# Odd layer of a two-layer backbone: three projection blocks take the scaled input before its norm, and the norm factor and shift are applied to their products

## Chip, core and metric

The kernel runs on one core of one Trainium2 chip. The core has five engines that each work through a queue of their own in a fixed order: PE (TensorE, matrix products), DVE (VectorE), ACT (ScalarE), POOL (GpSimd) and SP (SyncE, which here issues the DMAs). The metric is the time of one execution on the device in microseconds (us). Before the change the median of three runs is 2517.13 us; the runs lie between 2510.89 and 2518.06 us.

## What is computed

The model has two layers over 512 latent tokens and 256 context tokens with 2048 features. Only the odd layer's entry is touched. There the reference normalises every token, scales and shifts it with vectors that come from a conditioning input, and projects it:

```python
def rmsnorm(x, g):
    xf = x.astype(jnp.float32)
    y = xf * lax.rsqrt(jnp.mean(xf * xf, axis=-1, keepdims=True) + EPS)
    return (y * g.astype(jnp.float32)).astype(x.dtype)
...
h = rmsnorm(x, norm_g[l]) * (1.0 + scale) + shift
hc = rmsnorm(cx, norm_g[l]) * (1.0 + cscale) + cshift
...
u = h @ o_w_in[i]
uc = hc @ o_w_in[i]
```

The projections feed attention (mixer C: q and k with a norm per head and rotary angles; mixer D: low-rank attention), a SiLU gate, an output projection and a gated residual add. A final RMSNorm ends the model.

Since the norm factor is one number for each token, and the shift one vector for each of the two token groups, a projection can also be written as: norm factor times (scaled input times weight), plus (shift times weight).

## The kernel before

Features lie on the 128 partitions, tokens along the free axis (768 columns: 512 latent, 256 context). The 2048 features make 16 chunks `k`. Each float32 operand of a product is split into a high part, rounded to the type float32r, and the low rest; a product is three matmuls: high by high (L275), low input by high weight (L276), high input by low weight (L278). A weight block of 128 columns arrives as `wraw`; ACT casts it to `wh` (L256), and DVE subtracts to get `wl` (L215).

**End of the even layer.** `out_chunk` (L652 on) takes each finished block of the output projection, adds the residual on DVE (L656, L657, tile `nx`), squares it on ACT (L664), sums the squares on POOL (L669, `acc1`), multiplies it with the odd layer's scale on DVE (L666), and stores it to memory as `xad[k]` (L667). So `xad` holds the scaled input of the odd layer, not yet normalised.

**Norm factor.** `rstd_cols` (L240 products with ones on PE, L244 square root on ACT, L245 reciprocal on DVE) and `spread` (L220 on PE, L227 copies on DVE) turn the sums of squares into `rs1`, the factor of each token, on all partitions.

**First three blocks.** The loop over `k` at L700 loads `xad[k]` back as `xk` (L702) and calls `make_h` (L343): `xn = xk * rs1` (L345; on DVE for every third chunk, else on POOL), `h`, the rounded `xn + shift` (L350 on ACT, one instruction for latent and one for context), and `l`, the rest (L356 on DVE, again two). The pairs `h`, `l` of all chunks stay in `hT`, from which all later projections of the layer read. Within the same loop PE forms three blocks from each chunk as it comes: head group 0's key (K0) and value (V0), each with 512 latent and 256 context columns, and query head 0 (Q0), latent only. Their products stand in three J banks and in the S banks.

**Behind them.** K0's products are squared (ACT, L770 and L771), a norm factor of their own is formed (L240, L244, L245, L220) and applied (L782), then come rotary angles (L398, L399 on DVE, L400, L401 on POOL) and a split into `kh`, `kl`. V0 is transposed on PE (L450). Q0 goes the way of K0. Attention begins with the score products (L470, L474). PE fills gaps there with the next projections (a SiLU gate), which read `hT`.

Beside this, `mod_later` forms modulation vectors for the end of the layer: it loads `mraw`, and DVE adds up `macc` (L170, 15 instructions in this part of the program).

**What sets the order.** A scheduler lays out the program by a timeline that it simulates itself when the kernel is built. What it decides is one fixed order for each engine; on the chip an engine takes its instructions in that order and waits where an operand is missing. Tiles come from pools: `s3` has 11 buffers (`xk`, `xh`, `xl`, `nx`, `res` and others share them), `tm` has 3 (`xn`), J has 3 banks, T has 2.

Of the kernel before, what the change touches and what calls it, by code (L numbers as in the profile page):

```python
# [9 lines left out]
F32 = mybir.dt.float32  # L10
F32R = mybir.dt.float32r
AF = mybir.ActivationFunctionType
ALU = mybir.AluOpType
# [4 lines left out]
P = 128  # L18
D_MODEL = 2048
NCH = D_MODEL // P  # L20
SEQ = 512
CTX = 256
TOK = SEQ + CTX
# [18 lines left out]
def trunk_kernel(ctx: ExitStack, tc: tile.TileContext, T):  # L42
    nc = tc.nc
# [5 lines left out]
    sm = ctx.enter_context(tc.tile_pool(name="sm", bufs=6))  # L49
    dr = ctx.enter_context(tc.tile_pool(name="dr", bufs=1, space=DRAM))  # L50
    psj = ctx.enter_context(tc.tile_pool(name="psj", bufs=3, space=PSUM))
# [5 lines left out]
    sp = {}  # L57
# [5 lines left out]
        return pss.tile([P, 1024], F32, tag="S", name="S")  # L63

    def slot(name):
        return sp["s3"].tile([P, TOK], F32, tag="s3", name=name)

    def slotr(name):
        return sp["s3"].tile([P, TOK], F32R, tag="s3", name=name)

    def oslot(name):
        return sp["s3"].tile([P, TOK], F32, tag="o", name=name, bufs=2)
# [11 lines left out]
    xad = [dr.tile([P, TOK], F32, name=f"xad{j}") for j in range(NCH)]  # L84
# [15 lines left out]
    tp = pst.tile([P, 512], F32, name="T")  # L100
    nc.tensor.transpose(out=tp[:, :NV1], in_=vrow[:NV1, 0:P], identity=ident[:NV1, :NV1])
    nc.vector.tensor_copy(vcol, tp[:, :NV1])
    tp = pst.tile([P, 512], F32, name="T")
# [16 lines left out]
    modc = [const.tile([P, 3 * NCH, 2], F32, name=f"modc{l}") for l in range(2)]  # L120
# [71 lines left out]
    hT = []  # L192

    last_x = None
# [19 lines left out]
    def sub(o, a, h):  # L214
        nc.vector.tensor_tensor(o, a, h.bitcast(F32), op=ALU.subtract)  # L215
# [4 lines left out]
            nc.tensor.matmul(dst[:, P * i:P * i + P], lhsT=cols[:, 2 * t:2 * t + 1].broadcast_to([P, P]), rhs=ident,  # L220
                             start=True, stop=True)

    def spread(cols, dst):
        for ts in ((0, 1, 2, 3), (4, 5)):
            tp = psj.tile([P, 512], F32, name="J")
            spread_to(tp, cols, ts)
            nc.vector.tensor_copy(dst[:, P * ts[0]:P * ts[-1] + P], tp[:, :P * len(ts)])  # L227

    def jbank():
        return psj.tile([P, 512], F32, name="J")  # L230

    def tbank():
        return pst.tile([P, 512], F32, name="T")

    def rstd_cols(accs, ts, dim, name, bank=jbank):

        mp = bank()
        steps = [(a, t) for a in accs for t in ts]
        for i, (a, t) in enumerate(steps):
            nc.tensor.matmul(mp[:, 2 * t:2 * t + 2], lhsT=a[:, P * t:P * t + P], rhs=ones[:, 0:2],  # L240
                             start=(i == 0), stop=(i == len(steps) - 1))
        rs = sm.tile([P, 12], F32, name=name, bufs=2)
        n = 2 * len(ts)
        nc.scalar.activation(rs[:, :n], mp[:, :n], AF.Sqrt, bias=epsc, scale=1.0 / dim)  # L244
        nc.vector.reciprocal(rs[:, :n], rs[:, :n])  # L245
        return rs


    def wsplit(rv, nk):

        res = []
        for k0 in range(0, nk, 4):
            n = min(4, nk - k0)
            wh = wp.tile([P, 4, P], F32R, name="wh", bufs=4)
            wl = wp.tile([P, 4, P], F32R, name="wl", bufs=4)
            nc.scalar.copy(wh[:, :n, :], rv[:, k0:k0 + n, :])  # L256
            sub(wl[:, :n, :], rv[:, k0:k0 + n, :], wh[:, :n, :])
            res += [(wh[:, i, :], wl[:, i, :]) for i in range(n)]
        return res

    def wraw(w, col, k0, nk, raw=None):

        if raw is None:
            raw = wp.tile([P, 1024], F32, name="wraw", bufs=3)
        nc.sync.dma_start(raw[:, :nk * P], w[col // P][:, k0 * P:(k0 + nk) * P])
        return raw[:, :nk * P].rearrange("p (k c) -> p k c", k=nk)

    def mm_step(lat, cx, wk, xk, first, last, opens=True, closes=True, at=(0, 512)):


        wh, wl = wk
        xh, xl = xk
        regs = [(lat, *at)] + ([(cx, 512, 768)] if cx is not None else [])
        for o, c0, c1 in regs:
            nc.tensor.matmul(o, lhsT=wh, rhs=xh[:, c0:c1], start=first and (opens or o is lat), stop=False)  # L275
            nc.tensor.matmul(o, lhsT=wh, rhs=xl[:, c0:c1], start=False, stop=False)  # L276
        for o, c0, c1 in regs:
            nc.tensor.matmul(o, lhsT=wl, rhs=xh[:, c0:c1], start=False, stop=last and (closes or o is lat))  # L278
# [16 lines left out]
    for k in range(NCH):  # L295
# [3 lines left out]
        sq = ss if k == 0 else sp["ep"].tile([P, TOK], F32, name="e")  # L299
# [63 lines left out]
    w = T["ew"]  # L363
    s_start = sbanks()
# [38 lines left out]
    def etile(name):  # L403
        return sp["ep"].tile([P, TOK], F32, tag="e", name=name)
# [281 lines left out]
    for j in range(NCH):  # L686
# [4 lines left out]


    w = T["ow"]
    rs1 = etile("rs1")
    spread(rstd_cols((acc1, sq), range(6), D_MODEL, "rsx"), rs1)
    s_start = sbanks()
    odd_cols = (C_K0, C_V0, C_Q0)
    odd_ps = [(psj.tile([P, 512], F32, name="J"), s_start[:, 256 * i:256 * i + 256] if i < 2 else None)
              for i in range(3)]
    for k in range(NCH):  # L700
        xk = slot("xk")
        last_x = nc.sync.dma_start(xk, xad[k])  # L702
        hT[k] = make_h(1, k, xk, rs1, tmp("xn"), "mod")
        for i, (lat, cx) in enumerate(odd_ps):
            if k % 4 == 0:
                ws4[i] = wsplit(wraw(w, odd_cols[i], k, 4), 4)
            mm_step(lat, cx, ws4[i][k % 4], hT[k], k == 0, k == NCH - 1, opens=(i % 2 == 0), closes=(i % 2 == 1))

    def scaled(cols, f):
        nc.vector.tensor_scalar(cols[:, :8], cols[:, :8], f, None, op0=ALU.mult)  # L710
# [329 lines left out]
```

## Time and profile before

| what | value |
|---|---|
| median of the runs shown | 2517.13 us (2510.89 to 2518.06) |
| profiled execution, its own time | 2510.88 us |
| its span, first to last instruction | 2508.9 us |
| DVE, ACT, POOL busy | 1574.6, 1011.5, 248.9 us |
| DMA | 297.47 MB, mean 119 GB/s |

The span is the time from the profile's first instruction to its last; 2.0 us of the execution's own time lie around it. The clock that the throttle granted to PE is 0.985 on average. A row of the timeline has the start in us from the span's start, the length in us, engine, line, operation, what it writes and reads, how many instructions were merged, and in brackets how long the engine sat idle before it and what released it. A row of the groups has the shapes, the count, the summed busy time in us and the mean in ns, and behind the bar the idle time before them. A row by windows has a stretch, its length, and for each engine the busy time and the number of instructions; at the end stand the granted PE clock as a share of full speed, the busy share of the DMA engines and GB/s.

### The profile page before, as it was taken

Reading aid. Unit: us, or ns where it says so; the run is one execution under the profiler, and the core shown is the slowest. Engines: PE = TensorE matmul, PEld = TensorE weight load, DVE = VectorE, ACT = ScalarE, POOL = GpSimd, SP = SyncE. Lnnn points to the kernel's source line nnn. Section 1 sums busy time; section 2 is a strip of 40 time slices with the busy share of each in tenths; the row PEclk is TensorE's granted clock in tenths of the full one; section 3 lists DMA queues with packets and bytes.
Section 4 is the critical chain, followed back from the end, with each engine's and each line's share of the span. In section 5 each row is a group of like instructions: output and inputs, shape, how many; then the busy total and the mean of one; then the engine's idle time right before and its main releaser. Section 6 shows DMA issues by size and latency. Waiting matters only on the chain.

```text
span 2508.9 us, 36275 instructions
## 1 busy us (share of the span) xinstructions
PE 2408.6 (96%) x14214; PEld 2077.9 (83%) x14214; DVE 1574.6 (63%) x2795; ACT 1011.5 (40%) x1963; POOL 248.9 (10%) x160
## 2 busy tenths in 40 slices
PE   4899999999999999999989999899999999999998
PEld 2667888888888899989878888788888888888787
DVE  5377667656955787887466664757545335776534
ACT  3234454544444334324342222344434334554434
POOL 1111001001000101010001012300001011000010
PEclk9899999999999999999999999899999999999999
DMA  8762111111311343453425555425422221122234
GB/s 325 259 229 76 43 56 57 49 57 57 118 58 66 102 148 108 143 165 112 133 96 202 183 171 191 138 93 196 145 72 85 70 94 64 55 93 69 96 118 151
DMA packets 99082, 297.47 MB, mean 119 GB/s; under 512 B 11616, under 2 KB 12640, under 8 KB 98912
## 3 DMA queue, kind: packets, MB, share of 16 engines
q1 hardware_dynamic: 98912, 295.16, 34.7%
q8 instruction: 112, 1.84, 0.3%
q14 instruction: 58, 0.48, 0.1%
HBM read 269.16 MB, written 25.95 MB: 118 GB/s over the span
## 4 chain that ended last, share of the span: by engine, by line
PE 88%; DVE 5%; DMA 3%; issue 2%; ACT 1%; SPq 0%; ACTq 0%; DVEq 0%
PE J L275 22%; PE J L276 22%; PE J L278 22%; PE O L532 6%; PE S L474 4%; PE T L517 3%; PE S L470 3%; DMA mraw<-in_wm_dram 2%; DVE macc L170 1%; PE T L144 1%; PE J L178 1%; DVE l L356 1%; DVE wl L215 1%; PE T L240 1%; PE T L220 1%
## 5 line engine op out<-in xcount | busy, mean ns | idle before, releaser
L275 PE MATMUL J<-h,wh 128*128 128x512 f32 (+1 forms) x2224 | 786.0, 357 | 18.7 <-ACT h L350 11.8
L276 PE MATMUL J<-l,wh 128*128 128x512 f32 (+1 forms) x2224 | 766.8, 355 | 2.9 <-DVE l L356 1.8
L278 PE MATMUL J<-h,wl 128*128 128x512 f32 (+1 forms) x2224 | 706.6, 355 | 6.2 <-DVE wl L215 6.2
L256 ACT CAST wh<-wraw 128x512 fp32r<-128x512 f32 x492 | 303.9, 620 | 693.9 <-PE J L276 589.2
L215 DVE TENSOR_TENSOR wl<-wraw,wh 128x512 fp32r<-128x512 f32 x500 | 362.6, 729 | 338.7 <-ACT wh L256 325.2
L275 PEld LDWEIGHTS J<-h,wh 128*128 128x128 f32 x2224 | 421.2, 190 | 98.4 <-ACT h L350 12.9
L276 PEld LDWEIGHTS J<-l,wh 128*128 128x128 f32 x2224 | 423.5, 190 | 61.5 <-DVE l L356 3.5
L278 PEld LDWEIGHTS J<-h,wl 128*128 128x128 f32 x2224 | 388.3, 191 | 41.3 <-DVE wl L215 7.7
L170 DVE SCALAR_TENSOR_TENSOR macc<-mraw,silc,macc 128x512 f32<-128x512 f32 x420 | 319.7, 792 | 28.6 <-DMA mraw<-in_wm_dram 26.2
L275 PE MATMUL J<-yh,wh 128*128 128x512 f32 (+1 forms) x800 | 276.1, 351 | 5.1 <-ACT yh L438 5.1
L276 PE MATMUL J<-yl,wh 128*128 128x512 f32 (+1 forms) x800 | 272.2, 350 | 1.1 <-DVE yl L215 0.9
L486 DVE TENSOR_REDUCE nb<-S 128x1 f32<-128x768 f32 (+3 forms) x208 | 166.2, 799 | 146.8 <-PE S L474 79.2
L278 PE MATMUL J<-yh,wl 128*128 128x512 f32 (+1 forms) x800 | 254.1, 349 | 0.0
L521 ACT CAST pth<-T 128x256 fp32r<-128x256 f32 (+2 forms) x288 | 125.3, 451 | 188.2 <-PE T L517 185.1
L275 PEld LDWEIGHTS J<-yh,wh 128*128 128x128 f32 x800 | 150.1, 189 | 32.1 <-ACT yh L438 5.9
L215 DVE TENSOR_TENSOR ptl<-T,pth 128x256 fp32r<-128x256 f32 (+2 forms) x288 | 144.2, 514 | 51.6 <-ACT pth L521 49.9
L276 PEld LDWEIGHTS J<-yl,wh 128*128 128x128 f32 x800 | 150.7, 189 | 22.5 <-DVE yl L215 3.3
L493 ACT ACTIVATE e<-S,nb 128x256 f32<-128x256 f32 (+3 forms) x144 | 104.4, 725 | 154.2 <-DVE nb L486 88.0
L278 PEld LDWEIGHTS J<-yh,wl 128*128 128x128 f32 x800 | 140.6, 189 | 12.6
L400 POOL TENSOR_TENSOR r<-r,cos 128x512 f32<-128x512 f32 x31 | 44.4, 1431 | 792.4 <-DVE t L399 737.7
L517 PE MATMUL T<-identr,e 128*128 128x128 f32 x784 | 115.5, 274 | 2.9 <-DVE e L503 2.6
L517 PEld LDWEIGHTS T<-identr,e 128*128 128x128 f32 x784 | 94.6, 141 | 16.6 <-issue 2.6
(283 smaller groups left out, 3137.5 us busy)
## 6 DMA issues: line engine op xcount, KB each, us to landing
mraw<-in_wm_dram SPq DMA_DIRECT2D x128, 512.0 KB, 3.6
wraw<-in_ew_dram SPq DMA_DIRECT2D x96, 512.0 KB, 3.5
wraw<-in_ow_dram SPq DMA_DIRECT2D x64, 512.0 KB, 3.6
wraw<-in_wo_dram SPq DMA_DIRECT2D x62, 512.0 KB, 3.8
mraw<-in_wm_dram SPq DMA_DIRECT2D x80, 384.0 KB, 7.4
xT<-in_xT_dram SPq DMA_DIRECT2D x16, 384.0 KB, 7.3
res<-in_xT_dram SPq DMA_DIRECT2D x16, 384.0 KB, 4.5
xad<-nx SPq DMA_DIRECT2D x16, 384.0 KB, 2.5
```

What stands on the lines that cost most here:

```text
L170: nc.vector.scalar_tensor_tensor(macc[:, v, :], rv[:, i, :], sc, macc[:, v, :], op0=ALU.mult, op1=ALU.add)
L215: nc.vector.tensor_tensor(o, a, h.bitcast(F32), op=ALU.subtract)
L256: nc.scalar.copy(wh[:, :n, :], rv[:, k0:k0 + n, :])
L275: nc.tensor.matmul(o, lhsT=wh, rhs=xh[:, c0:c1], start=first and (opens or o is lat), stop=False)
L276: nc.tensor.matmul(o, lhsT=wh, rhs=xl[:, c0:c1], start=False, stop=False)
L278: nc.tensor.matmul(o, lhsT=wl, rhs=xh[:, c0:c1], start=False, stop=last and (closes or o is lat))
L474: nc.tensor.matmul(S[:, 512:end], lhsT=q, rhs=k[:, 128 * lo:128 * hi], start=(i == 0), stop=(i == n - 1 and not masks))
L486: nc.vector.tensor_reduce(nb, S, axis=AX.X, op=ALU.max, negate=True)
L493: nc.scalar.activation(e, S, AF.Exp, bias=nb, scale=1.0 if scale is None else scale, accum_out=den)
L517: nc.tensor.transpose(out=tp[:, 128 * (b - b0):128 * (b - b0) + 128], in_=e[:, 128 * b:128 * b + 128], identity=ident)
L521: nc.scalar.copy(ph, tv)
L532: nc.tensor.matmul(o, lhsT=v[:, cols[i]], rhs=pt[part][:, i, :], start=(n == 0), stop=(n == len(steps) - 1))
```

## The change

The loop over `k` is split in two. The first loop reads `xad[k]` into a tile of 770 columns: 512 latent ones, then two columns that take the chunk's shift for latent and context from `modc`, then 256 context ones. The tile is split into `xh` and `xl` without norm and shift, and the three blocks are formed from these. The two extra columns of the product are shift times weight. Q0 gets the two columns in a T bank and is therefore formed as 256 and 258 columns. Behind the loop `rs1` is formed with T banks, and a new function `late_norm` multiplies each block by `rs1` on DVE out of the bank into an SBUF tile `first` and adds the shift's product on ACT. The second loop loads every `xad[k]` again and calls `make_h`, since all later projections still read `hT`; it forms no products.

```diff
+    def slot2(name, dt=F32):
+        return sp["s3"].tile([P, TOK + 2], dt, tag="s3", name=name)
...
-    spread(rstd_cols((acc1, sq), range(6), D_MODEL, "rsx"), rs1)
     s_start = sbanks()
     odd_cols = (C_K0, C_V0, C_Q0)
-    odd_ps = [(psj.tile([P, 512], F32, name="J"), s_start[:, 256 * i:256 * i + 256] if i < 2 else None)
-              for i in range(3)]
+    first_ps = [jbank() for _ in range(3)]
+    q_bank = tbank()
+    for k in range(NCH):
+        xk = slot2("xk")
+        last_x = nc.sync.dma_start(xk[:, 0:512], xad[k][:, 0:512])
+        nc.sync.dma_start(xk[:, 514:770], xad[k][:, 512:768])
+        nc.vector.tensor_copy(xk[:, 512:514], modc[1][:, k, :])
+        xh, xl = slot2("xh", F32R), slot2("xl", F32R)
+        nc.scalar.copy(xh, xk)
+        sub(xl, xk, xh)
+        for i in range(3):
+            if k % 4 == 0:
+                ws4[i] = wsplit(wraw(w, odd_cols[i], k, 4), 4)
+            wh, wl = ws4[i][k % 4]
+            if i < 2:
+                regs = ((first_ps[i], 0, 512), (s_start[:, 512 * i:512 * i + 258], 512, 770))
+            else:
+                regs = ((first_ps[i][:, 0:256], 0, 256), (q_bank[:, 0:258], 256, 514))
+            for n, (wk, xx) in enumerate(((wh, xh), (wh, xl), (wl, xh))):
+                for o, c0, c1 in regs:
+                    nc.tensor.matmul(o, lhsT=wk, rhs=xx[:, c0:c1], start=(k == 0 and n == 0),
+                                     stop=(k == NCH - 1 and n == 2))
+    spread(rstd_cols((acc1, sq), range(6), D_MODEL, "rsx", tbank), rs1, tbank)
+
+    def late_norm(name, parts, bias):
+        t = slot(name)
+        bc = sm.tile([P, 2], F32, name="bc", bufs=3)
+        nc.vector.tensor_copy(bc, bias)
+        for ps, c0, c1, v in parts:
+            nc.vector.tensor_tensor(t[:, c0:c1], ps, rs1[:, c0:c1], op=ALU.mult)
+            nc.scalar.activation(t[:, c0:c1], t[:, c0:c1], AF.Identity, bias=bc[:, v:v + 1])
+        return t
...
     for k in range(NCH):
         xk = slot("xk")
-        last_x = nc.sync.dma_start(xk, xad[k])
+        nc.sync.dma_start(xk, xad[k])
         hT[k] = make_h(1, k, xk, rs1, tmp("xn"), "mod")
-        for i, (lat, cx) in enumerate(odd_ps):
-            if k % 4 == 0:
-                ws4[i] = wsplit(wraw(w, odd_cols[i], k, 4), 4)
-            mm_step(lat, cx, ws4[i][k % 4], hT[k], k == 0, k == NCH - 1, opens=(i % 2 == 0), closes=(i % 2 == 1))
```

All tiles of `s3` grow by two columns. Up to the last chunk of the even layer the order of every engine is what it was. In the changed file the lines of functions ahead of this place stand three further down (L356 is now L359), those behind it 40 further down (L770 is now L810).

On DVE before, this is what stands between the last piece `l` of the sixteen chunks and the reciprocal (L245) for K0's own norm:

```order
L356 SCALAR_TENSOR_TENSOR l_15_15283<-xn,modc_194,h_15_15282 128x512
L356 SCALAR_TENSOR_TENSOR l_15_15283<-xn,modc_194,h_15_15282 128x256
L170 SCALAR_TENSOR_TENSOR macc<-mraw,silc,macc 128x512 x3
L215 TENSOR_TENSOR wl<-wraw,wh 128x512
L170 SCALAR_TENSOR_TENSOR macc<-mraw,silc,macc 128x512
L215 TENSOR_TENSOR wl<-wraw,wh 128x512 x2
L170 SCALAR_TENSOR_TENSOR macc<-mraw,silc,macc 128x512 x6
L215 TENSOR_TENSOR wl<-wraw,wh 128x512 x3
L245 RECIPROCAL rsx<-rsx 128x12
L782 TENSOR_TENSOR ev<-ev,T 128x512
```

On DVE after the change, the same reciprocal (now L248) stands behind the new multiplications (L732) and behind all sixteen `l`; the first gap leaves out the other multiplications and small rows, the second the `l` of the chunks between, five more `xn` and seven `macc`:

```order
L218 TENSOR_TENSOR xl<-xk,xh 128x770
...
L732 TENSOR_TENSOR first<-T,rs_14800 128x256
L173 SCALAR_TENSOR_TENSOR macc<-mraw,silc,macc 128x512
L218 TENSOR_TENSOR wl<-wraw,wh 128x512
L348 TENSOR_TENSOR xn<-xk,rs_14800 128x768
L173 SCALAR_TENSOR_TENSOR macc<-mraw,silc,macc 128x512 x2
L359 SCALAR_TENSOR_TENSOR l_0_15346<-xn,modc_194,h_0_15345 128x512
...
L359 SCALAR_TENSOR_TENSOR l_15_15496<-xn,modc_194,h_15_15495 128x256
L173 SCALAR_TENSOR_TENSOR macc<-mraw,silc,macc 128x512 x2
L248 RECIPROCAL rsx<-rsx 128x12
```

The sixteen pieces have moved from among the three blocks' products to behind them, and stay ahead of K0's norm.

On ACT after the change, the squares of K0 (L810, L811) stand behind all of `h`, and these behind the added shift (L733); the left-out rows are the `h` between:

```order
L733 ACTIVATE first<-first,bc 128x512
L733 ACTIVATE first<-first,bc 128x256 x3
L353 ACTIVATE h_0_15345<-xn,modc_194 128x512
...
L353 ACTIVATE h_15_15495<-xn,modc_194 128x256
L810 ACTIVATE sq<-first 128x512
L811 ACTIVATE sq<-first 128x256
L814 ACTIVATE ev<-first,vcol 128x512
```

Before, the squares stood behind all of `h` as well, but with no `L733`, and the products ran between.

On PE after the change, this is the end of the first loop's products (L722) and what follows:

```order
L722 MATMUL J<-xh,wl 128x256
L722 MATMUL T<-xh,wl 128x258
L243 MATMUL T<-ones,sq 128x2 x6
L223 MATMUL T<-identr,rsx 128x128 x6
L453 MATMUL J<-identr,ev 128x128 x6
L278 MATMUL J<-h_0_15345,wh 128x512
L279 MATMUL J<-l_0_15346,wh 128x512
```

Between the last product and K0's norm (L243, L223) nothing else stands on PE. Before, these rows followed the last of the blocks' products (L278) in the same way.

More of the change, by code (lines that the diff above doesn't have):

```diff
@@ L65, in slot @@
     def slot(name):
-        return sp["s3"].tile([P, TOK], F32, tag="s3", name=name)
+        return sp["s3"].tile([P, TOK + 2], F32, tag="s3", name=name)[:, :TOK]
+    def slot2(name, dt=F32):
+        return sp["s3"].tile([P, TOK + 2], dt, tag="s3", name=name)
     def slotr(name):
-        return sp["s3"].tile([P, TOK], F32R, tag="s3", name=name)
+        return sp["s3"].tile([P, TOK + 2], F32R, tag="s3", name=name)[:, :TOK]
     def oslot(name):
@@ L221, in spread_to, with spread @@
                              start=True, stop=True)
-    def spread(cols, dst):
+    def spread(cols, dst, bank=None):
         for ts in ((0, 1, 2, 3), (4, 5)):
-            tp = psj.tile([P, 512], F32, name="J")
+            tp = (bank or jbank)()
             spread_to(tp, cols, ts)
@@ new lines, in trunk_kernel @@
+    spread(rstd_cols((acc1, sq), range(6), D_MODEL, "rsx", tbank), rs1, tbank)
[7 more added lines that the diff above has]
+        return t
+    odd_ps = []
+    for i in range(2):
+        cx = s_start[:, 512 * i:512 * i + 258]
+        t = late_norm("first", ((first_ps[i], 0, 512, 0), (cx[:, 2:258], 512, 768, 1)), cx[:, 0:2])
+        odd_ps.append((t[:, :512], t[:, 512:768]))
@@ L700, in trunk_kernel @@
+    t = late_norm("first", ((first_ps[2][:, 0:256], 0, 256, 0), (q_bank[:, 0:256], 256, 512, 0)), q_bank[:, 256:258])
+    odd_ps.append((t[:, :512], None))
     for k in range(NCH):
         xk = slot("xk")
-        last_x = nc.sync.dma_start(xk, xad[k])
+        nc.sync.dma_start(xk, xad[k])
         hT[k] = make_h(1, k, xk, rs1, tmp("xn"), "mod")
-        for i, (lat, cx) in enumerate(odd_ps):
-            if k % 4 == 0:
-                ws4[i] = wsplit(wraw(w, odd_cols[i], k, 4), 4)
-            mm_step(lat, cx, ws4[i][k % 4], hT[k], k == 0, k == NCH - 1, opens=(i % 2 == 0), closes=(i % 2 == 1))
```

## The prediction

> **What bounds the kernel now.** I read the page's busy lines first, then a table by windows around the odd layer's entry, then the timeline there.
>
> ```profile
> PE 2408.6 (96%) x14214; PEld 2077.9 (83%) x14214; DVE 1574.6 (63%) x2795; ACT 1011.5 (40%) x1963; POOL 248.9 (10%) x160
> ...
> 1546.50:1556.00 9.50, 5.80 (x38) 5.33 (x36) 4.72 (x9) 2.27 (x5) 1.58 (x1) 0.82 0.93 324
> 1556.00:1613.00 57.00, 52.28 (x240) 42.39 (x241) 50.86 (x59) 25.37 (x47) 21.73 (x10) 0.88 0.56 195
> 1613.00:1640.00 27.00, 22.36 (x103) 18.83 (x102) 13.78 (x25) 10.49 (x21) 5.89 (x4) 0.81 0.30 98
> 1640.00:1660.00 20.00, 20.00 (x111) 17.28 (x110) 10.99 (x21) 7.99 (x16) 0.00 (x0) 1.00 0.26 93
> ```
>
> Over the span PE is the bound, with about 100 us idle (span 2508.9 less 2408.6). From 1640 on it is full, with DVE at half. Between 1556 and 1613 the picture differs: 240 matmuls (the three blocks, 15 for each of 16 chunks) take 57 us while DVE is busy 50.86. At PE's own pace they would take less:
>
> ```profile
> 1562.46 0.39 PE L276 MATMUL J<-l,wh 128*128 128x512 f32 x1
> 1562.69 0.40 PE L278 MATMUL J<-h,wl 128*128 128x512 f32 x1
> ...
> 1561.39 0.28 PE L278 MATMUL S<-h,wl 128*128 128x256 f32 x1
> 1561.51 0.28 PE L275 MATMUL S<-h,wh 128*128 128x256 f32 x1
> ```
>
> From start to start a 512-wide matmul costs 0.23 us and a 256-wide one 0.12. A chunk is 9 of the one and 6 of the other, 2.8 us, and sixteen are 44.5 us. So 12.5 us of this stretch are lost, and more ahead of it and behind it:
>
> ```profile
> 1546.48 1.40 PE L240 MATMUL J<-ones,acc 128*128 128x2 f32 x12
> 1547.80 0.84 ACT L664 ACTIVATE sq<-nx 128x768 f32<-128x768 f32 x1 [0.85 <-DVE nx L657]
> 1548.69 1.50 PE L240 MATMUL J<-ones,sq 128*128 128x2 f32 x12 [0.82 <-ACT sq L664]
> 1550.81 2.93 PE L220 MATMUL J<-identr,rsx 128*128 128x128 f32 x12 [0.62 <-DVE rsx L245]
> 1553.78 0.42 DVE L227 COPY rs<-J 128x256 f32<-128x256 f32 x1 [0.16 <-PE J L220]
> 1556.06 0.96 PE L275 MATMUL J<-h,wh 128*128 128x512 f32 x3 [2.32 <-ACT h L350]
> ...
> 1612.86 0.39 PE L278 MATMUL J<-h,wl 128*128 128x512 f32 x1
> 1613.09 1.40 PE L240 MATMUL T<-ones,sq 128*128 128x2 f32 x12
> 1617.26 0.22 DVE L245 RECIPROCAL rsx<-rsx 128x12 f32<-128x12 f32 x1
> 1617.54 2.93 PE L220 MATMUL T<-identr,rsx 128*128 128x128 f32 x12 [3.05 <-DVE rsx L245]
> ...
> 1633.67 0.28 PE L470 MATMUL S<-kh,qh 128*128 128x256 f32 x1
> ```
>
> The even layer's last product ends at 1546.5. The norm's chain (square, L240, L245, L220, L227, `xn`, `h`) holds the blocks up until 1556.06; they end at 1613, and K0's own norm reaches PE at 1617.54. I measure the change at this last event: ahead of the entry nothing moves, and behind it the work is the same. Removing the norm from the blocks' way addresses a real loss. The question is what stands in its place.
>
> **The first pass.** PE's work for a chunk becomes 6 matmuls of 512 columns and 12 of 256 or 258: 6 x 0.23 + 12 x 0.12 = 2.8 us, 45 us for sixteen, as before. It needs no `rs1`, only a load, a cast and a subtraction, whose nearest rows are these:
>
> ```profile
> 1625.17 0.84 ACT L438 CAST kh<-ev 128x768 fp32r<-128x768 f32 x1 [0.68 <-POOL ev L401]
> 1626.67 0.95 DVE L215 TENSOR_TENSOR kl<-ev,kh 128x768 fp32r<-128x768 f32 x1
> 1603.83 0.68 DVE L215 TENSOR_TENSOR wl<-wraw,wh 128x512 fp32r<-128x512 f32 x1
> 1626.59 0.17 DVE L710 TENSOR_SCALAR qsc<-qsc 128x8 f32<-128x8 f32 x1
> xk<-xad SPq DMA_DIRECT2D x16, 384.0 KB, 5.3
> ```
>
> For a chunk DVE gives 0.95 to `xl`, at most 0.17 to the two shift columns (the row is for 8, so 0 to 0.17), and 12 x 0.68 / 16 = 0.5 to `wl`: 1.6 us; ACT gives 0.84 and about as much as DVE for `wh`: 1.3. Both stay under PE's 2.8, so they hide behind it, and so does the load: 384 KB and a sixteenth of 3 MB of weights in 2.8 us is about 210 GB/s, where the window from 1546.5 shows 324. PE becomes the bound of this pass. The first `xh` stands on ACT behind the square that ends at 1548.64 (1547.80 + 0.84), so products begin at about 1549.5 instead of 1556.06.
>
> To the 45 us come the norm's own 24 + 12 small matmuls, now inside the pass: 1.40 + 1.50 + 2.93 = 5.8. The start is not smooth: chunk 1's second load stands on SP behind the store of the last `xad`, and PE's clock is low after a pause. Before, the first 4.3 us carried 11 matmuls, where full pace carries 19. I add 3 us for that (bounds 0 and 5), and 2 for waits at the three places where weights change (before, one such wait was 1.74). The last product ends at 1549.5 + 45 + 5.8 + 3 + 2, about **1605** (1599 to 1612), against 1613.
>
> **The second pass, which has lost its cover.** Before, the sixteen `h`, `l` pairs ran beside the blocks' products. Now the first loop gives PE its 45 us without them, and they stand behind `late_norm` and ahead of K0's norm, on DVE and on ACT both. On PE nothing stands between the last product and K0's norm. So PE waits for the whole pass. Its length is the main term:
>
> ```profile
> 1556.04 4.07 DVE L356 SCALAR_TENSOR_TENSOR l<-xn,modc,h 128x512 fp32r<-128x512 f32 x3 [0.79 <-ACT h L350]
> 1599.31 0.73 DVE L170 SCALAR_TENSOR_TENSOR macc<-mraw,silc,macc 128x512 f32<-128x512 f32 x1
> ```
>
> From the first `l` (1556.04) to the end of the last (1599.31) DVE took 43.3 us and was never idle for long. In that stretch, by windows of one line each (in this order L356, L345, L170, L215):
>
> ```profile
> 1556.00:1599.30 43.30, 31.14 (x32) 0.84 0.51 180
> 1556.00:1599.30 43.30, 4.73 (x5) 0.84 0.51 180
> 1556.00:1599.30 43.30, 5.24 (x5) 0.84 0.51 180
> 1556.00:1599.30 43.30, 3.98 (x6) 0.84 0.51 180
> ```
>
> The changed order has the same 32 `l` and 5 `xn` there, no `wl`, and 7 `macc` instead of 5. So 43.3 - 4.0 + 2 x 0.74 = 40.8 us. Ahead of the first `l`, behind the last product, stand two `wl`, one `first` of 256 columns, three `macc` and one `xn`, and the tiny copy:
>
> ```profile
> 1619.65 0.69 DVE L782 TENSOR_TENSOR ev<-ev,T 128x512 f32<-128x512 f32 x1 [2.17 <-PE T L220]
> 1620.51 0.42 DVE L782 TENSOR_TENSOR ev<-ev,T 128x256 f32<-128x256 f32 x1 [0.17 <-PE T L220]
> 1611.46 1.54 DVE L170 SCALAR_TENSOR_TENSOR macc<-mraw,silc,macc 128x512 f32<-128x512 f32 x2 [3.63 <-DMA mraw<-in_wm_dram]
> ```
>
> 2 x 0.68 + 0.42 + 3 x 0.75 + 0.95 + 0.1 = 5.1. The other multiplications of `late_norm` (0.69 and 0.42 each, as the L782 rows that also read a bank) fall in the last product's shadow, and its additions run on ACT ahead of `h`, beside DVE's rows. Behind the last `l` come two `macc`, 1.5, then the reciprocal, 0.2. K0's square and sums take ACT and PE some 3 us after the last `h`, which ends before the last `l` does; they fit in these. Together 5.1 + 40.8 + 1.5 + 0.2 = **47.6 us** from the last product to K0's L220. The second loads issue some chunks ahead, as buffers come free; I cost them at nothing, covered by `late_norm`, and if that cover fails they cost one landing, 5.3 us by the row above. The same holds for a late `mraw` (3.63 by its row); the 15 `macc` were all ahead of this event before, too.
>
> How sure are 40.8? The range of one `l`, and POOL's `xn`:
>
> ```profile
> L356 DVE SCALAR_TENSOR_TENSOR l<-xn,modc,h x32: 466/739/2337, 1556.0 to 1598.9; 128x512 fp32r<-128x512 f32 x16, 128x256 fp32r<-128x256 f32 x16
> L345 POOL TENSOR_TENSOR xn<-xk,rs x10: 2209/2238/2785, 1554.4 to 1589.1; 128x768 f32<-128x768 f32 x10
> ```
>
> Alone, a pair costs 0.74 + 0.47 = 1.21, and sixteen 19.4; they took 31.1. The slow ones fall on POOL's ten `xn`, 11.7 us in all, 1.2 for each. If none met POOL, the stretch would be 40.8 - 11.7 = 29.1; that is the lower end. The upper end is 40.8 + 5.3 + 3.6 = 49.7. I take 40.8, the nearest: same instructions, same partners.
>
> The Trainium skill, page "SBUF — State Buffer", section "SBUF: two separate sides", says that a DVE instruction with two SBUF inputs and a GpSimd instruction take a shared port pair as a lock, and the loser waits for the whole of the other. By that rule each of ten `xn` could cost DVE its full length, and the stretch would be 10 to 11 us longer and the net +42 or +43; the trace shows locking (an `l` of 2337 ns beside an `xn` of 2238) but half the sum, so I stay with the row.
>
> **Sum.** K0's L220 begins at 1605 + 47.6 = 1652.6 instead of 1617.54: +35.1. From there to the first score product PE had 16.1 us (1633.67 - 1617.54) for 59 matmuls, which would take 33 x 0.23 + 26 x 0.12 = 10.7. The new order puts 54 gate products there instead of 33, so the chain through K0 and Q0 is covered better; about 3 us of that loss return. Net **+32 us**. On the profiled execution's own 2510.88 us that is 2543; on the median shown, 2517.13, which lies 6.2 higher with the same kernel, 2549. I take 2546.
>
> **Rivals.**
>
> *Faster, by about 10 us.* DVE works 1.6 of each 2.8 us in the first pass, so it has some 19 us free, more while PE starts. If the second pass ran in that gap, the last product near 1605 would be followed by K0's norm after 4 us as before (1613.0 to 1617.54): 1609.5, -8, and -11 with the better tail. It decides at a pass of 12 us behind the last product. Against it: DVE's order has every `l` behind the last `xl`, an engine keeps its order, and 16 uncovered pairs alone are 19.4.
>
> *The pass is cheap, +8 to +22.* POOL can be up to three `xn` ahead, and if the locking largely goes, the wait falls to 29.1 + 6.8 = 35.9, and with the end at 1599 K0's L220 starts at 1635: +17, less 3.
>
> *The first pass is starved, +44 to +65.* If its operands come late, PE stops often, and runs slowly after each stop:
>
> ```profile
> 1587.37 0.50 PE L275 MATMUL J<-h,wh 128*128 128x512 f32 x1 [1.74 <-ACT wh L256]
> 1588.60:1598.20 9.60, 8.62 (x24) 6.42 (x25) 9.60 (x14) 3.14 (x6) 2.21 (x1) 0.50 0.43 122
> ```
>
> After this stop the granted clock was 0.50 for 9.6 us, which cost 4.8. Three to five such spells put the last product at 1620 to 1630, and the whole at +47 to +57. By the Trainium skill, page "TensorE: Matmul & The Clock Gate", section "🔬 Part 1: The HAM clock gate (the "warmup" mystery)", an idle window of about 3.4 us drops the clock to half, and about 3.4 us of work restore it; that would be 1.7 us a spell, +37 to +41. The row, a shorter stop and a longer spell, speaks for the dearer price.
>
> *The change does not do what it says, +40.* If products do not start before the norm is there, the last one stays near 1613 and the pass comes on top: 1613 + 47.6 - 1617.5 - 3 = +40. Against it: none of their operands reads `rs1`.
>
> **How the numbers follow.** Forecast (+23 to +44, the last rival in it) 0.75; cheap pass 0.09; starved 0.11; near zero 0.03; faster 0.02. A measurement of this kernel tells about 0.3% from no change, 7.5 us. Faster by more 0.02, within 0.03, slower by more 0.95. The low end, 2528, is +17 on 2510.9, inside the cheap pass; the high end, 2567, is +50 on 2517.1, inside the starved one. What lies beyond both is under 0.2.
>
> **What would show it.** The first L722 should start near 1549.5 and the last end near 1605, with a clock near 1.0 between. Then a gap on PE of 40 to 50 us ahead of L223, released by DVE's L248; in it DVE full with L359, and PE's idle over the span up by about 32. I would be wrong if `l` ran at 1.2 us a pair beside POOL, if L722 were slower than 0.23 and 0.12, or if the gap were filled by projections.

## The result, and the profile after

The changed kernel takes 2552.64 us (median of 4 runs, 2549.17 to 2555.22), the kernel before 2515.06 beside it (4 runs): ratio 1.0141, 95% interval 1.0122 to 1.0160, 37.6 us slower. The forecast was 2546, range 2528 to 2567. The profiled execution of after took 2555.22 us, the longest of its four, that of before 2510.88, the shortest of its own; so the two traces lie 44.3 us apart, and the forecast from trace to trace is the +32.

First the page's busy line, then TensorE's (PE's) waits from 1545 to 1680 (what waited, for whom; total us, times, longest):

```profile
PE 2407.1 (94%) x14262; PEld 2082.5 (82%) x14262; DVE 1599.1 (63%) x2836; ACT 1028.1 (40%) x1985; POOL 247.6 (10%) x160
```

```profile
PE T L243 <- ACT sq L810: 45.8, 1, 45.8
PE J L722 <- ACT xh L710: 7.0, 4, 2.8
PE T L223 <- DVE rsx L248: 2.3, 1, 2.3
```

PE's idle time over the span rose from 100 to 146 us (2553.4 less 2407.1), and one wait holds 45.8 of it. Its place, in the timeline:

```profile
1548.35 0.51 PE L281 MATMUL J<-yh,wl 128*128 128x512 f32 x2
...
1551.71 0.50 PE L722 MATMUL J<-xh,wh 128*128 128x512 f32 x1 [2.85 <-ACT xh L710]
...
1611.30 0.28 PE L722 MATMUL T<-xh,wl 128*128 128x258 f32 x1
1657.40 2.72 PE L243 MATMUL T<-ones,sq 128*128 128x2 f32 x12 [45.82 <-ACT sq L810]
1662.44 2.90 PE L223 MATMUL T<-identr,rsx 128*128 128x128 f32 x12 [2.32 <-DVE rsx L248]
...
1679.08 0.28 PE L473 MATMUL S<-kh,qh 128*128 128x256 f32 x1
```

The even layer's last row starts at 1548.35, where before it started at 1546.12 (quoted below): a drift of 2.2 us that the change has no part in. The first product of the odd layer's three blocks follows as soon as the raw input is split. The last one stands at 1611.30, and then PE has nothing until K0's norm. By windows (for PE, weight load, DVE, ACT, POOL; then the granted clock):

```profile
1556.00:1570.00 14.00, 14.00 (x80) 12.74 (x81) 6.29 (x12) 6.00 (x9) 0.00 (x0) 0.85 0.34 109
1570.00:1590.00 20.00, 19.47 (x125) 17.50 (x124) 9.21 (x18) 5.92 (x8) 0.00 (x0) 1.00 0.69 220
1590.00:1606.00 16.00, 12.34 (x65) 10.57 (x64) 6.05 (x11) 5.15 (x8) 0.00 (x0) 0.89 0.58 209
1606.00:1655.00 49.00, 5.58 (x36) 4.87 (x34) 46.41 (x56) 22.60 (x41) 22.29 (x10) 0.59 0.57 204
```

The long wait ends with ACT's squares of K0 (L810), which stand behind all `h` in ACT's order. In that window ACT is busy for 22.60 of 49 us and DVE for 46.41, so DVE, which makes `l` and some of the `xn` for `h`, is the engine that is full. The two resources of this region have been put one behind the other: while the products run, VectorE (DVE) is busy for 38 to 46% of each window, and while DVE makes `l`, PE is idle. Before, both ran from 1556 to 1613 together (52.28 and 50.86 of 57 us).

To compare kernels below I read three distances in each trace: from the start of the even layer's last row to that of the blocks' last product (A), from there to K0's L223 (L220 before; B), and on to the first score product (C). For before these are its rows:

```profile
1546.12 0.52 PE L278 MATMUL J<-yh,wl 128*128 128x512 f32 x2
...
1612.86 0.39 PE L278 MATMUL J<-h,wl 128*128 128x512 f32 x1
```

With 1617.54 and 1633.67 that is A 66.7, B 4.7, C 16.1. After: A 62.95, B 51.1, C 16.6. The sum is 43.2 us longer; the drift of 2.2 ahead and -0.9 behind the first score (2553.4 - 1679.08 against 2508.9 - 1633.67) make the 44.5 us of the spans.

### The profile page after: what moved, and what is told of

It is laid out like the page before. It is cut to its first block, busy times and chain, and to the rows that moved or that the text cites. A ratio compares the mean times of both kernels' runs of the same rounds, so it can differ in the third digit from the quotient of the medians.

```text
span 2553.4 us, 36527 instructions
## 1 busy us (share of the span) xinstructions
PE 2407.1 (94%) x14262; PEld 2082.5 (82%) x14262; DVE 1599.1 (63%) x2836; ACT 1028.1 (40%) x1985; POOL 247.6 (10%) x160
## 4 chain that ended last, share of the span: by engine, by line
PE 85%; DVE 6%; DMA 5%; ACT 2%; issue 2%; SPq 0%; ACTq 0%; DVEq 0%
PE J L278 21%; PE J L279 21%; PE J L281 21%; PE O L535 5%; PE S L477 4%; DMA mraw<-in_wm_dram 3%; PE T L520 3%; PE S L473 3%; DVE macc L173 1%; DVE l L359 1%; PE T L243 1%; DVE wl L218 1%; PE J L722 1%; PE J L181 1%; PE T L147 1%
## 5 line engine op out<-in xcount | busy, mean ns | idle before, releaser
L278 PE MATMUL J<-h,wh 128*128 128x512 f32 (+1 forms) x2176 | 766.8, 355 | 14.2 <-ACT h L353 9.9
L279 PE MATMUL J<-l,wh 128*128 128x512 f32 (+1 forms) x2176 | 744.4, 352 | 0.9 <-DVE l L218 0.9
L281 PE MATMUL J<-h,wl 128*128 128x512 f32 (+1 forms) x2176 | 684.0, 353 | 6.0 <-DVE wl L218 6.0
L278 PEld LDWEIGHTS J<-h,wh 128*128 128x128 f32 x2176 | 411.3, 190 | 91.4 <-ACT h L353 10.7
L279 PEld LDWEIGHTS J<-l,wh 128*128 128x128 f32 x2176 | 413.0, 190 | 55.8 <-DVE l L218 2.3
L281 PEld LDWEIGHTS J<-h,wl 128*128 128x128 f32 x2176 | 377.7, 190 | 38.5 <-DVE wl L218 6.6
L278 PE MATMUL J<-yh,wh 128*128 128x512 f32 (+1 forms) x800 | 276.9, 352 | 4.3 <-ACT yh L441 4.3
L278 PEld LDWEIGHTS J<-yh,wh 128*128 128x128 f32 x800 | 150.7, 189 | 31.4 <-ACT yh L441 5.2
L218 DVE TENSOR_TENSOR ptl<-T,pth 128x256 fp32r<-128x256 f32 (+2 forms) x288 | 144.2, 514 | 51.1 <-ACT pth L524 49.7
L281 PEld LDWEIGHTS J<-yh,wl 128*128 128x128 f32 x800 | 141.0, 190 | 12.6
L403 POOL TENSOR_TENSOR r<-r,cos 128x512 f32<-128x512 f32 x31 | 44.3, 1430 | 792.2 <-DVE t L402 734.9
```

## The experiments

Medians in us; the ratio is to the kernel before beside them (its medians in four sets: 2515.06, 2516.01, 2515.33, 2514.2); A, B, C as above.

| kernel | median | ratio, 95% | A | B | C |
|---|---|---|---|---|---|
| after | 2552.64 | 1.0122 to 1.0160 | 63.0 | 51.1 | 16.6 |
| a_half | 2535.17 | 1.0058 to 1.0092 | 64.8 | 28.1 | 18.5 |
| a_late_macc | 2545.42 | 1.0095 to 1.0133 | 64.7 | 42.3 | 16.2 |
| a_no_pool | 2547.98 | 1.0104 to 1.0140 | 64.8 | 44.1 | 18.9 |
| a_act_queue | 2551.27 | 1.0121 to 1.0154 | 71.7 | 41.6 | 17.1 |
| a_pool_queue | 2552.75 | 1.0123 to 1.0170 | 68.6 | 42.3 | 18.6 |
| a_k_first | 2549.12 | 1.0108 to 1.0146 | 63.4 | 8.8 | 16.2 |
| k_late_macc | 2539.56 | 1.0075 to 1.0119 | 63.3 | 7.0 | 13.4 |
| a_one_loop | 2546.18 | 1.0104 to 1.0141 | 94.9 | 7.7 | 20.5 |
| o_reuse | 2526.66 | 1.0032 to 1.0060 | 76.3 | 7.7 | 20.0 |
| b_late_macc | 2512.28 | 0.9979 to 0.9999 | 65.7 | 2.6 | 14.8 |
| b_both | 2506.93 | 0.9951 to 0.9977 | 56.9 | 2.7 | 15.7 |
| b_no_pool | 2501.63 | 0.9929 to 0.9965 | 56.8 | 2.8 | 15.7 |

**Is it the second pass? a_half.** The second loop makes only the first eight chunks of `h` and `l`; the products behind it read these in place of the other eight.

```diff
     for k in range(NCH):
+        if k >= 8:
+            hT[k] = hT[k - 8]
+            continue
         xk = slot("xk")
```

> The second loop of the changed kernel makes only the first 8 of 16 chunks of h and l; the other 8 are taken from chunk k-8, so half of that pass is left out and the products behind it use wrong operands of the same size. Theory (PE waits for the whole second pass, which DVE sets): 16 of 32 l and half of xn leave the wait; they are about 36 us of DVE time for all, so the wait ahead of L243 falls from 45.8 to about 28 us and the time by about 18 us against the changed kernel (2552.6), to about 2535. Rival (the wait is set by the second loads or by K0's own chain): the wait and the time fall by less than 5 us.

2535.17, where expected. The long wait fell from 45.8 to 24.1 us:

```profile
PE T L243 <- ACT sq L813: 24.1, 1, 24.1
```

So half of the pass is worth 21.7 us of this wait and 17.5 us of the time, 2.2 us a chunk. C grew by 1.8. A, ahead of the pass, is 64.8 against 63.0, though PE, DVE and ACT run the first loop in the same order in both: by so much single traces differ. The pass is on the path, at about four fifths of the wait's price.

**What fills it? a_late_macc and a_no_pool.** One holds back the weight sums of `mod_later` (`macc`), which DVE makes between the chunks; the other takes GpSimd (POOL) out of the odd layer's `xn`.

```diff
-            tick(3.5)
+            tick(3.5 if h else 0)
             finish(1, h, o, sg, 512)
-            tick(3.5)
+            tick(3.5 if h else 0)
...
-            nc.sync.dma_start(sgd[h], sg[:, :512])
+            st = nc.sync.dma_start(sgd[h], sg[:, :512])
+            if h == 0:
+                last_x = st
```

> The changed kernel with the sums of mod_later for the end of the layer held back until the first gate of head 0 is stored (no ticks in head 0, loads ordered behind that store). Theory (the wait is a sum of DVE's instructions): 12 macc between the last product and K0's reciprocal leave it, 0.75 us each and two of about 2, and one wait of 1.24 for their load: the wait falls by 9 to 13 us and the time to about 2541 to 2544, since DVE is half idle where they go. Rival (ACT's h or POOL's xn set the pace, macc only fills gaps): the time stays within 3 us of 2552.6.

2545.42: 7.2 less, a little short of the expected. PE's long wait is 38.6 us, also 7.2 less, and B is 8.8 shorter. A is 1.8 longer, but it is that in a_half and a_no_pool too, so this says nothing about the edit.

```diff
-        (nc.gpsimd if k % 3 else nc.vector).tensor_tensor(xn, xk, rs, op=ALU.mult)
+        (nc.gpsimd if k % 3 and l == 0 else nc.vector).tensor_tensor(xn, xk, rs, op=ALU.mult)
```

> The changed kernel with all sixteen xn of the odd layer on DVE, none on POOL. Theory (an l is slow only because POOL's xn holds it up): all l run at 0.74 and 0.47 us, 19.4 us in all instead of about 31, while DVE takes ten more xn of 0.95, 9.5 us: net about -2 us against 2552.6, and no l over 0.8 us. Rival (the slow l have another cause, such as waiting for ACT's h): l stays at about 31 us, and the time rises by about 9 us.

4.7 less, where about 2 were expected. By the spread of the four runs of each kernel, this step and that of a_late_macc are known to within about 4 us either way. DVE's groups from 1606 to 1660 (summed busy us, mean ns of one), in after and then in a_no_pool:

```profile
L359 DVE SCALAR_TENSOR_TENSOR l<-xn,modc,h 128x512 fp32r<-128x512 f32 x16 | 19.6, 1223 | 0.0
L173 DVE SCALAR_TENSOR_TENSOR macc<-mraw,silc,macc 128x512 f32<-128x512 f32 x13 | 12.3, 949 | 0.0
L359 DVE SCALAR_TENSOR_TENSOR l<-xn,modc,h 128x256 fp32r<-128x256 f32 x16 | 10.7, 667 | 0.0
L348 DVE TENSOR_TENSOR xn<-xk,rs 128x768 f32<-128x768 f32 x6 | 5.7, 946 | 0.0
L218 DVE TENSOR_TENSOR wl<-wraw,wh 128x512 fp32r<-128x512 f32 x3 | 3.6, 1215 | 0.0
```

```profile
L348 DVE TENSOR_TENSOR xn<-xk,rs 128x768 f32<-128x768 f32 x16 | 14.9, 966 | 0.0
L359 DVE SCALAR_TENSOR_TENSOR l<-xn,modc,h 128x512 fp32r<-128x512 f32 x16 | 12.2, 760 | 0.1
L173 DVE SCALAR_TENSOR_TENSOR macc<-mraw,silc,macc 128x512 f32<-128x512 f32 x15 | 11.4, 757 | 0.0
L359 DVE SCALAR_TENSOR_TENSOR l<-xn,modc,h 128x256 fp32r<-128x256 f32 x16 | 7.9, 493 | 0.0
L218 DVE TENSOR_TENSOR wl<-wraw,wh 128x512 fp32r<-128x512 f32 x3 | 2.1, 685 | 0.0
```

Without POOL's ten `xn` the `l` take 20.1 us instead of 30.3, each `macc` 0.19 less (2.5 over 13) and the three `wl` 1.5 less: 14.2 us in all, of which DVE gives 9.2 back for ten more `xn`. The net of 5.0 is near the measured 4.7, though the distances share it out otherwise (B 7.0 shorter, A and C together 4.1 longer). The Trainium skill, page "SBUF — State Buffer", section "SBUF: two separate sides", has whichever of the two engines starts first hold the shared ports for its whole instruction. The runs agree in kind: DVE lost 14.2 us to 22.29 us of POOL, more than `l` alone shows and less than all of it.

**Are late loads what slowed the first pass? a_act_queue and a_pool_queue.** In after the first pass's loads have gaps on SyncE's (SP's) queue:

```profile
1585.19 0.38 SPq L706 DMA_DIRECT2D xk<-xad  x1
1585.61 0.43 SPq L707 DMA_DIRECT2D xk<-xad  x1
1595.26 0.33 SPq L268 DMA_DIRECT2D wraw<-in_ow_dram  x1
1595.69 0.38 SPq L706 DMA_DIRECT2D xk<-xad  x1
```

For 9 us nothing is issued; then a weight load goes, and the chunk's load right behind it. Either that weight load held up the chunks, or they would have had to wait for buffers anyway. Both kernels move the two loads of a chunk to another queue (`nc.scalar`, `nc.gpsimd`):

```diff
-        last_x = nc.sync.dma_start(xk[:, 0:512], xad[k][:, 0:512])
-        nc.sync.dma_start(xk[:, 514:770], xad[k][:, 512:768])
+        last_x = nc.scalar.dma_start(xk[:, 0:512], xad[k][:, 0:512])
+        nc.scalar.dma_start(xk[:, 514:770], xad[k][:, 512:768])
```

> The changed kernel with the 32 loads of the first loop issued from ACT's queue instead of SP's. Theory (in the first pass PE's 7.0 us of waits for xh come from loads that stand on SP behind weight loads for which no buffer is free yet): the waits for xh nearly vanish, the last product ends 4 to 7 us earlier, and the time falls to about 2546 to 2549. Rival 1 (the tile buffers come free too late): no change. Rival 2 (32 issues of about 0.4 us take ACT's time and delay its casts): the pass gets longer by some us.

> The changed kernel, with the first loop's two loads per chunk issued from GpSimd's queue instead of SP's, where they stand behind no weight load that waits for a buffer. Theory 1, head of line on SP: TensorE's 7.0 us of waits for xh fall to 2 or less and the last product comes near 1606: 2546 to 2549, unless the weight sums take the place, as in a_act_queue (2551.3). Theory 2, the loads wait for their own buffers (11 of one ring) or take their time on the wire: the waits stay at 5 to 8 us and the time within 2 us of 2552.6.

Neither is faster than after by more than its interval, but the edit did more than move these loads. In both kernels SP issues the `mraw` loads ahead of the first pass (in a_act_queue the last at 1554.96, in after they begin at 1599.30), and every `macc` of this stretch runs before the first pass begins, none between the chunks of the second. B is 9.5 and 8.8 us shorter, about as in a_late_macc. In return the sums, waiting for their loads, stand on DVE ahead of the even layer's last block, and the first product of the pass starts 9.7 and 11.4 us behind the start of that layer's last row, in after 3.4. In a_act_queue:

```profile
1551.80 0.75 DVE L173 SCALAR_TENSOR_TENSOR macc<-mraw,silc,macc 128x512 f32<-128x512 f32 x1 [1.93 <-DMA mraw<-in_wm_dram]
1552.47 0.74 DVE L659 SCALAR_TENSOR_TENSOR nx<-J,modc,res 128x512 f32<-128x512 f32 x1
```

So the two times say little about the loads. PE's waits for `xh` say more, in a_act_queue and then in a_pool_queue:

```profile
PE J L722 <- ACT xh L710: 14.9, 6, 9.2
```

```profile
PE J L722 <- ACT xh L710: 13.4, 3, 10.9
```

The longest of each is the late start (in after 2.8). The others sum to 5.7 and 2.5 us, in after to 4.2, and from its first product to its last the pass takes 62.0 and 57.2 us, in after 59.6 (in a_half and a_no_pool 61.4). On ACT's queue a load is issued behind a cast that itself waits for a load:

```profile
1559.70 0.83 ACT L710 CAST xh<-xk 128x770 fp32r<-128x770 f32 x1 [4.37 <-DMA xk<-xad]
1559.71 0.33 ACTq L706 DMA_DIRECT2D xk<-xad  x1
```

On POOL's queue the loads say what they wait for, from 1580 on:

```profile
1580.22 0.54 POOL L706 DMA_DIRECT2D xk<-xad  x1 [10.34 <-PE T L722]
1583.83 0.54 POOL L706 DMA_DIRECT2D xk<-xad  x1 [2.54 <-PE T L722]
```

Each waits for products, that is, for a buffer that these free, in the ring of 11, three for each chunk. So the weight loads ahead of them on SP may have cost the pass some 2 to 4 us (57.2 against 59.6 and 61.4), and the buffers hold up the loads as well. What a larger ring would bring, no run here shows.

**Can the pass be covered later? a_k_first and k_late_macc.** The second loop is written behind the preparation of K0, V0 and Q0; k_late_macc adds the held sums.

```diff
-    for k in range(NCH):
-        xk = slot("xk")
-        nc.sync.dma_start(xk, xad[k])
-        hT[k] = make_h(1, k, xk, rs1, tmp("xn"), "mod")
+    def second_pass():
...
             qh, ql = split(ev, 512, slotr, "q")
+            if h == 0:
+                second_pass()
```

> The changed kernel with its second loop written behind the preparation of K0, V0 and Q0, ahead of head 0's attention. In the order that results, K0's reciprocal stands on DVE ahead of all sixteen l, and PE's row has head 0's scores and two gate blocks, chunk by chunk, beside the pass. Theory (the loss is PE's row having nothing beside the pass, not the pass itself): the one wait of 45.8 us breaks up; DVE still needs about 68 us for the pass and head 0's softmax, in which PE now finds some 38 us of work, so the time falls by 15 to 22 us against 2552.6, to 2531 to 2538, still above the kernel before, since DVE stays the bound. Rival (the pass itself, with its second loads, is the cost, wherever it stands): less than 5 us.

2549.12, a miss by 11 us or more: 3.5 less than after, inside the rival's window. B is down to 8.8, but the time came back behind it. SP's queue:

```profile
1621.91 20.81 SPq L166 DMA_DIRECT2D mraw<-in_wm_dram  x6
1642.77 27.63 SPq L747 DMA_DIRECT2D xk<-xad  x14
```

The second loads stood behind six `mraw` loads, and the `macc` fed by these stood among K0's own chain on DVE. That gave a new theory, which k_late_macc was to decide:

> The second loop written behind the preparation of K0, V0 and Q0, as in a_k_first (2549.1), and the weight sums of mod_later held until head 0's gate has been stored, as in a_late_macc. Theory 1, loads in SP's order: in a_k_first the second loop's loads stood behind the mraw loads on SP's queue (issued at 1642.8 only, xn from 1647.1), so the pass began 30 us late; with mraw gone they are issued near 1620 and the pass runs under the preparation and the scores: 2520 to 2532. Theory 2, VectorE is short: the pass's 40 us and the preparation and softmax of head 0 share one engine whatever the loads do, so only the 7.2 us return that the held sums gave in a_late_macc: 2540 to 2546.

2539.56, 0.4 under the second theory's window: the loads theory fails. Its condition came true (the second loads were issued from 1616.44 on), but the first `xn` still ran at 1634.50. By windows in k_late_macc:

```profile
1612.00:1645.00 33.00, 17.89 (x67) 14.68 (x66) 20.87 (x37) 17.61 (x35) 12.21 (x7) 0.55 0.42 140
1645.00:1700.00 55.00, 48.86 (x230) 38.83 (x230) 48.67 (x69) 31.38 (x58) 18.79 (x11) 0.96 0.42 133
```

DVE is idle for 12 of the first 33 us, because in its order the pass stands behind the whole preparation, whose rows wait for one another; then it is nearly full. PE, which waits for the same preparation, has a granted clock of 0.55. Beside a_late_macc (2545.42), moving the pass is worth 5.9 us (1.8 of them lie between the kernels before of the two sets): the one long wait has become many short ones.

**Can it be covered by the products? a_one_loop and o_reuse.** Here the norm is formed ahead, and `make_h` stands in the first loop.

```diff
+    spread(rstd_cols((acc1, sq), range(6), D_MODEL, "rsx", tbank), rs1, tbank)
     for k in range(NCH):
         xk = slot2("xk")
...
+        xr = slot("xk")
+        nc.sync.dma_start(xr, xad[k])
+        hT[k] = make_h(1, k, xr, rs1, tmp("xn"), "mod")
```

> The changed kernel with the norm factor formed ahead of the first loop and make_h called inside it for each chunk (second load kept), so that products and pieces run side by side again; the three blocks still take the input without its norm. Theory (the loss is the lost cover): no wait of 40 us ahead of L243; DVE has per chunk 0.96 + 0.16 for the new operands on top of what it had before, 18 us over sixteen, and becomes the bound of the loop again, starting about 6 us earlier: the time is that of the kernel before plus 8 to 16 us, 2524 to 2532, some 20 to 28 below the changed kernel. Rival (the new operands themselves slow the products): the time stays above 2540.

2546.18, another miss, with the time that the rival names. From 1552 to 1645:

```profile
1552.00:1645.00 93.00, 62.51 (x300) 52.96 (x299) 59.23 (x88) 37.23 (x62) 21.17 (x10) 0.82 0.55 188
```

Neither engine is full: the loop waits for something else. PE's wait for `xh`, and one of those on ACT behind it:

```profile
PE J L723 <- ACT xh L711: 23.4, 10, 6.4
```

```profile
1580.99 0.83 ACT L711 CAST xh<-xk 128x770 fp32r<-128x770 f32 x1 [6.10 <-DMA xk<-xad]
```

The loop waits for loads. o_reuse takes the second load away and makes `xn` from the tile that was split (the columns 0 to 512 and 514 to 770 of `xk`, in two instructions):

```diff
-        xr = slot("xk")
-        nc.sync.dma_start(xr, xad[k])
-        hT[k] = make_h(1, k, xr, rs1, tmp("xn"), "mod")
+        hT[k] = make_h(1, k, xk, rs1, tmp("xn"), "mod")
```

> As a_one_loop (norm formed ahead, make_h of every chunk inside the first loop; 2546.2), but the chunk is not loaded a second time: xn is made from the tile that the products' split has read. 16 loads and 16 buffers fewer. Theory 1, loads and the 11 buffers: a_one_loop's loop took 92 us with VectorE busy for 59 of 93 only, because loads stood behind others that waited for buffers; without the second load the loop goes by VectorE's work and takes 66 to 70 us, its last product near 1620, and the time is 2518 to 2530. Theory 2, the chain of ScalarE, VectorE and GpSimd through each chunk and its tiles is what takes the time: the last product stays behind 1635, and the time at 2540 to 2548.

2526.66, inside the first theory's window, 19.5 us under a_one_loop; though A, 76.3 against 94.9, is longer than the 66 to 70 of that theory, and the loop does not go by DVE's work (58.76 of the 73 us from 1552 to 1625). The new operands are the same in both, so a_one_loop's rival, which blamed these, falls: the second load with its buffer was most of what held that loop, and of the change's 37.6 us all but 12.5 are gone. What is left shows in the three distances: A + B + C is 104.0, before 87.5, and the two profiled executions differ by the same 16.4 (2527.32 against 2510.88), which is in part chance: o_reuse reaches the even layer's last row 5.3 us later, and its time behind the first score is 5.3 us shorter. What this loop waits for, on PE from 1545 to 1660:

```profile
PE J L728 <- DVE xl L218: 10.2, 8, 2.1
PE J L728 <- ACT xh L716: 5.2, 4, 2.2
PE T L243 <- ACT sq L812: 4.0, 1, 4.0
```

The split of the raw chunk is work that before did not have, and `late_norm` stands ahead of K0's sums (the last row). With the pass covered, the change still only adds.

**The two parts on the kernel before.** The edits of a_late_macc and of a_no_pool, made to the kernel before, and both together:

> The kernel before, with the sums of mod_later for the end of the layer held back until head 0's first gate is stored, as in a_late_macc. Theory (DVE is the bound of the blocks' stretch before the change too): 5 macc, 5.2 us, leave the stretch from 1556 to 1599, and the waits for their loads behind it: the time falls by 3 to 7 us against the kernel before. Rival (PE or the norm's chain is the bound there): within 1.5 us of it.

> b_late_macc with all xn of the odd layer on DVE, none on POOL. Theory (POOL's xn hold up DVE's l for 11.7 us in all and save DVE only ten xn, 9.5 us): another 0 to 4 us below b_late_macc, and no l over 0.8 us. Rival (before the change POOL's help is worth it, since its xn come while PE has work): 3 us or more above b_late_macc.

> The kernel before, with the odd layer's xn all on VectorE and nothing else (b_both was this and the held sums: 2506.9, 8.4 us under before; the held sums alone 3). If the two parts add up: 2509 to 2512, about 5 us under before. If GpSimd's xn only hurt by sharing the time with the weight sums: within 2 us of before.

b_late_macc is 3.0 us under before, at the edge of what can be told; b_both 8.4 (5.4 under b_late_macc, where 0 to 4 were expected); b_no_pool 12.6, more than any expectation, and the fastest kernel here, 51.0 us under after. The two parts do not add up: A, B and C are alike in b_both and b_no_pool, and their ratios' intervals overlap, so no gain of the held sums shows once POOL is out. From the even layer's end to the last product, in before and in b_no_pool:

```profile
1546.50:1613.00 66.50, 58.08 (x278) 47.73 (x277) 55.58 (x68) 27.64 (x50) 23.31 (x10) 0.87 0.61 213
```

```profile
1548.90:1605.80 56.90, 52.58 (x281) 45.12 (x280) 49.21 (x78) 26.52 (x49) 0.00 (x0) 0.94 0.70 247
```

DVE does ten more instructions in 6.4 us less, and its idle time falls from 10.9 to 7.7; together the 9.6 us by which the stretch is shorter. DVE set the pace there already, and POOL's help was a loss.

## Why the prediction was right, point by point

The sign, the mechanism and the place were as predicted: PE runs out of work for a whole pass over 16 chunks, ahead of K0's norm (a_half takes half of the pass and half of the wait). By the prediction's own steps, on before's clock (after's less 2.2):

- **Start of the products.** Forecast 3.4 us behind the start of the even layer's last row (1549.5 less 1546.12); measured 3.4 (1551.71 less 1548.35).
- **Last product near 1605 (1599 to 1612).** Measured 1609.4 (1611.6 less 2.2): 4.4 late. The loads were not hidden: PE waited 7.0 us for `xh`, 2.8 at the start, which the start contains, and 4.2 in the loop, where the sum had 2 for waits of another kind. The step "they hide behind it, and so does the load" compared rates (210 GB/s against 324) and left out when a load can be issued. The rest fits the clock: 0.82 from 1549 to 1556, then 0.85, 1.00 and 0.89 by the windows above, which is an estimated 5 us lost (7 x 0.18 + 14 x 0.15 + 16 x 0.11) where the sum had 3.
- **47.6 us to K0's norm.** Measured 50.9 (1662.44 - 1611.58): 3.3 long. Its three terms, each with its rows:

```profile
1610.18 0.69 DVE L732 TENSOR_TENSOR first<-J,rs 128x512 f32<-128x512 f32 x1 [1.93 <-PE J L722]
...
1614.45 0.41 DVE L732 TENSOR_TENSOR first<-T,rs 128x256 f32<-128x256 f32 x1
1614.78 1.90 DVE L173 SCALAR_TENSOR_TENSOR macc<-mraw,silc,macc 128x512 f32<-128x512 f32 x1
1616.60 2.28 DVE L218 TENSOR_TENSOR wl<-wraw,wh 128x512 fp32r<-128x512 f32 x1
...
1621.12 2.20 DVE L359 SCALAR_TENSOR_TENSOR l<-xn,modc,h 128x512 fp32r<-128x512 f32 x4
...
1659.43 0.74 DVE L173 SCALAR_TENSOR_TENSOR macc<-mraw,silc,macc 128x512 f32<-128x512 f32 x1
1661.40 0.75 DVE L173 SCALAR_TENSOR_TENSOR macc<-mraw,silc,macc 128x512 f32<-128x512 f32 x1 [1.24 <-DMA mraw<-in_wm_dram]
1662.07 0.22 DVE L248 RECIPROCAL rsx<-rsx 128x12 f32<-128x12 f32 x1
```

  The front is 9.5 (1621.12 - 1611.58) instead of 5.1, for two reasons. The step by which the multiplications of `late_norm` "fall in the last product's shadow" failed: the first starts at 1610.18, after DVE has waited 1.93 us for its bank, and the other five stand behind the last product, where the sum had one; the 2.2 us up to 1613.78 are not in it. Then a `macc` of 1.90 and a `wl` of 2.28 (alone 0.75 and 0.68) met POOL's first `xn`, 2.7 us more than alone, so the lock that the prediction counted for `l` alone began here. The stretch is 38.3 (to 1659.43) instead of 40.8; its `l` took 30.3 us, in before 31.14, so the choice of before's row over 29.1 was right. The tail is 3.0 instead of 1.7: the late `mraw` that was costed at nothing cost 1.24.
- **"About 3 us of that loss return".** They did not: C is 16.6 against 16.1. The gaps were filled as forecast: PE was busy for 16.56 of the 16.60 us from 1662.40 on, with the 54 gate products, and before for 14.48 of the 16.10 from 1617.50 on. But the first score came no earlier, and behind it, where gate products done ahead would be saved, only 0.9 us went. Why no more, no run here isolates.

Of the signs that were named, the full DVE in the gap and the place came. The clock between was not near 1.0 throughout; the long wait ended with ACT's squares, and only the 2.3 us behind it with L248; and PE's idle time rose by 46 us instead of about 32.

The sum of the misses, 4.4 + 3.3 + 3.5, is the 11.2 us by which the trace's +43.2 exceeds +32; between the medians the difference is +37.6, 5.6 over. The stretch, 2.5 short, hides part of the misses in the front and the tail. The whole locks, for which the prediction names +42 or +43, meet the trace's +43.2 by chance: they would have made the stretch 10 to 11 us longer, and it was 2.5 shorter. The rivals fell: the products did not wait for the norm (its factor reached L223 at 1569.30, they began at 1551.71), nothing of the pass ran inside the first loop, the cheap pass would have needed a wait of 35.9, and the starved first pass a last product at 1620 or later.

## What to carry to other kernels

Work that shares a loop with products is covered only while it shares it: before splitting a loop, ask which engine was full in it (here DVE, 50.9 of 57 us), and whether the half that is moved still has something beside it. A helper engine that slows the one it helps may be a loss: compare an instruction's shortest row with its mean in that stretch. A rate that fits says little about loads; ask which buffer each waits for, and what stands ahead of it in its queue.

## What the runs showed of the hardware that was not expected

- POOL's elementwise work slowed DVE's instructions beside it: from 1606 to 1660 in after a `wl` took 1.215 us on average instead of 0.685, a `macc` 0.949 instead of 0.757, and in before an `l` of 512 columns up to 2.337 (alone 0.74). It was not only those with two SBUF inputs: in before the multiplication L666 with one input tensor (128x512) took 1.68 us beside POOL's sum of squares (1530.18 to 1532.13), and 0.41 without it. Taking ten POOL multiplications of 2.24 us out of before was worth 12.6 us.
- Many short waits went with a low granted clock, as one long wait did: 0.55 over 33 us in k_late_macc, where PE was busy for 17.89 of them and no wait was above 6.5 us, and 0.82 over 93 us in a_one_loop, without a wait above 6.4 us; in after 0.59 over the 49 us that hold the wait of 45.8.
- The even layer's last row, with the same work ahead of it, started anywhere from 1544.35 (a_no_pool) to 1552.51 us (b_both) after the first instruction; so single traces are compared by distances within them.
